# An HGRN2 trunk layer on one core: the prologue in two feature halves

## The chip, the core and the metric

The kernel runs on one core of a Trainium2 chip. The core has five engines with a queue of instructions each, worked off in order: TensorE (PE, matrix products and transposes into PSUM), VectorE (DVE, element-wise work and scans), ScalarE (ACT, activations and copies; it also issues some transfers), GpSimd (POOL, small element-wise work, memsets) and SyncE (SP, which issues transfers). The metric is the device time of one execution in microseconds, lower is better.

## The reference, cut to what matters

One layer: an HGRN2 mixer over 256 context tokens and 2048 latent tokens, then a gated ConvFFN, with adaLN modulation. The part that this case touches is the start:

```python
m_l = (silu(c) @ w_ada + b_ada)            # latent: shift, scale, gate, ... (6 x 1024)
m_c =  silu(c_ctx) @ w_ada + b_ada         # context
hl = rmsnorm(lat, norm_g0) * (1 + sc1) + sh1
hc = rmsnorm(cx,  norm_g0) * (1 + csc1) + csh1
q, f_fwd, f_bwd, v, g = split(h @ w_in)    # per head of 128 features, 8 heads
# f = lb + (1 - lb) * sigmoid(f): chunkwise linear recurrence, forward and backward;
# the latent scans start from the final state of the context scan
```

All is float32. A product is made of three fast ones: each operand is split into a rounded high part and the rest, and the kernel adds high x high, high x low and low x high.

## The kernel before, in words

The 2048 latent tokens lie in two halves of 1024 and each half in two units of 512 tokens (four tiles of 128). For each half the kernel goes over the eight heads. For a head it projects the context (in the first half only) and both units with five weight types: 2 and 1 are the gates of the two directions, 3 the values, 0 the queries, 4 the output gate. One `project` is eight feature blocks k of 128 with three products each (`step`, L442 to L448; high and low parts of the weight and of the tokens). Then come the mixer's end and the FFN, which the change leaves alone.

Before any projection the **prologue** (L200 to L309, in its own PSUM pool) makes what the projections read:

- 16 transfers of 512 KB bring the first 2048 columns of `w_ada` (shift and scale; tile `wada`), each 128 rows by 1024 columns; ACT's queue issues ten and SP's six (`ada_load`, L211). SP also brings two context tiles, the raw weights of the types (`raw`) and eight latent tiles (`x`; `stage` puts tile t into a buffer that is free by then).
- PE multiplies them with SiLU of both conditions (`silp`), 32 products in four column groups (L250, tile `mps`). ACT copies the sum (L256), PE turns it (L258, `mt`), and six small DVE instructions (L267 to L269) make the factors `A1` and shifts `B1`, for the context (index 1) and the latents (index 0).
- The normalised context is turned by PE, modulated half by ACT and half by DVE (`modulated`, L197 and L198), and split into high and low parts (`split`: ACT L78 writes the high part, DVE L79 the rest) into `cxt`.
- `normalize` of a latent tile: ACT squares and sums (L104), DVE scales (L74), POOL takes the root's inverse (L75), DVE multiplies (L109).

The first head (`head` with `first`) projects the context with types 2, 1 and 3. `unit_tok(u, k)` makes feature block k of unit u: four PE transposes, one modulation, one split into `tok`. The gates' projection of the first unit follows the blocks one by one; the second unit's tiles are normalised and its blocks are made at fixed ticks of a clock that counts steps (`at`). Then queries, values, the second unit's gates, and the first score products, ahead of which PE turns the factor `kd` (L592). I call that instruction **the meeting point**: in the program before and in the changed one the PE work ahead of it is the same work, and what follows it has the same order.

What sets the order: each engine's queue is fixed when the program is built, by the order of the code; `behind_of` keeps an instruction behind a named pair.

Of the kernel before, what the change touches and what calls it, by code (L numbers as in the profile page):

```python
# [11 lines left out]
F32 = mybir.dt.float32  # L12
# [33 lines left out]
def body(ctx, tc, a, out):  # L46
# [53 lines left out]
    def normalize(xt, junk, stp, on_act=False):  # L100

        ss = stp.tile([128, 1], F32, name="ss", tag="ss", bufs=2)
        rs = stp.tile([128, 1], F32, name="rs", tag="rs", bufs=2)
        act.activation(junk, xt, AF.Square, accum_out=ss)  # L104
        rms_scale(rs, ss, 1, D)
        if on_act:
            act.activation(xt, xt, AF.Copy, scale=rs)
        else:
            dve.tensor_scalar(xt, xt, rs, None, OP.mult)  # L109
# [69 lines left out]
    HEAD0 = (2, 1, 3, 0)  # L179
# [19 lines left out]

    with ExitStack() as c0:  # L200
        p0s = pool_(c0, "p0s", space=PSUM)
        silv = sil.rearrange("p (two k) -> p k two", two=2)
        silp = gp.tile([128, KT, 32], F32, name="silp", tag="kt", bufs=2)
        tps = [p0s.tile([128, 2, 2, 128], F32, name="tp", tag=f"tp{g}", bufs=1) for g in range(2)]
        mp = p0s.tile([128, 512], F32, name="mps")
        mt = p0s.tile([128, 4, 128], F32, name="mt")
        tps += [p0s.tile([128, 2, 2, 128], F32, name="tp", tag=f"tp{g}", bufs=1) for g in (2, 3)]
        ada = [place(i, [128, 4, D], F32, "wada") for i in range(4)]
        junk = lp.tile([128, D], F32, name="junk", tag="stg", bufs=1)

        def ada_load(q, k, i):  # L211
            n = 2 * k + i
            q.dma_start(ada[n // 4][:, n % 4], a["w_ada"][k * 128:(k + 1) * 128, i * D:(i + 1) * D])

        def raw_w(ty):
            raw = rawp.tile([128, D], F32, name="raw", tag="raw")
            sp.dma_start(raw, a["w_in"][0, ty])
            return raw

        head0 = {}  # L220

        def split_head0(ty, raw):
            head0[ty] = w = wp.tile([128, 2, KT, 128], F32R, name="w", tag="w")
            return split(w[:, 0], w[:, 1], raw.rearrange("p (k n) -> p k n", k=KT))

        pool.memset(silp, 0.0)
        stage(-2)
        stage(-1)
        for k in range(2):
            ada_load(act, k, 0)  # L230
            ada_load(sp, k, 1)
        act.activation(sil, vec[:, V_C:V_C + 16], AF.Sigmoid)
        dve.tensor_tensor(sil, sil, vec[:, V_C:V_C + 16], OP.mult)
        dve.tensor_copy(silp[:, :, 0:2], silv)
        head_raw = {}
        for k in range(2, KT):
            ada_load(act, k, 0)
            ada_load(act if k >= KT - 2 else sp, k, 1)
            if k == KT - 3:
                head_raw[2] = raw_w(2)  # L240
        head_raw[1] = raw_w(1)
        for t in range(4):
            stage(t)
        for t in (-2, -1):
            normalize(staged[t], junk, gp)
        late_junk = place(2, [128, D], F32, "junk")
        for k in range(KT):
            for c in range(4):
                n = 2 * k + c // 2
                pe.matmul(mp[32 * c:32 * c + 32], silp[:, k],  # L250
                          ada[n // 4][:, n % 4, c % 2 * 512:(c % 2 + 1) * 512],
                          start=k == 0, stop=k == KT - 1, skip_group_check=True)
        made = split_head0(2, head_raw[2])
        m2 = gp.tile([128, 512], F32, name="m2", tag="q", bufs=2)
        with behind_of(made):
            act.activation(m2, mp, AF.Copy)  # L256
        for j in range(4):
            pe.transpose(mt[:, j], m2[:, j * 128:(j + 1) * 128], ident)  # L258
        for g in range(4):
            turn_tok(tps[g], (-2, -1), (2 * g, 2 * g + 1))  # L260
        mv = mt.rearrange("p j (c r) -> p c j r", c=4)

        def by_k(v):
            return v.rearrange("p (c j) -> p c j", c=2)

        for i in (1, 0):
            dve.tensor_tensor(by_k(A1[i]), mv[:, 2:4, :, i], by_k(vec[:, V_BA + 8:V_BA + 16]), OP.add)  # L267
            dve.tensor_tensor(by_k(B1[i]), mv[:, 0:2, :, i], by_k(vec[:, V_BA:V_BA + 8]), OP.add)
            dve.scalar_tensor_tensor(A1[i], A1[i], 1.0, vec[:, V_NG:V_NG + 8], OP.add, OP.mult)  # L269
        hmc = [gp.tile([128, 2, 2, 128], F32, name="hm", tag="gv"[g % 2], bufs=2) for g in range(4)]  # L270

        def evict_ctx(g):
            return [modulated(hmc[g][:, i], tps[g][:, i], 2 * g + i, 1, i == 0).ins for i in range(2)]

        def split_ctx(g):
            b = cxt[:, g // 2, :, :, 2 * (g % 2):2 * (g % 2) + 2]
            return split(b[:, :, 0], b[:, :, 1], hmc[g].rearrange("p k s n -> p s k n"))
# [9 lines left out]
        for t in range(4, 8):  # L287
            stage(t)
# [1518 lines left out]
```

## Time and profile before

| | us |
|---|---|
| median of 3 runs (2755.13 to 2757.07) | 2755.96 |
| the profiled execution's own time | 2759.34 |
| its span, first to last instruction | 2757.3 |
| first context product (PE L445) | at 34.18 |
| meeting point (PE L592) | at 94.93 |

Times in the rows are microseconds from the span's start. A row of the timeline gives start, duration, engine, line, operation, output and inputs, sizes, how often, and in brackets the idle time of the engine just before with what ended it. PE's products overlap in its pipeline, so the distance of two starts, not the duration, is what one costs. The table of windows gives for each stretch its length, the busy time and count of PE, of its weight loads, DVE, ACT and POOL, PE's granted clock, the share of the transfer engines and GB/s.

### The profile page before, as it was taken

The numbers are of one execution on the slowest core, as the hardware profiler recorded it, in microseconds if no ns is written. First come the engines' busy times: TensorE is split into PE (matmuls) and PEld (weight loads), VectorE is DVE, ScalarE is ACT, GpSimd is POOL, SyncE is SP. The second block draws the span as 40 slices with busy tenths as digits, with TensorE's granted clock in tenths as the row PEclk, the third lists the DMA queues.
The fourth block names the chain that finished last, engine by engine and source line by source line (L and its number), as shares of the span: only waits on it lengthen the run. The fifth ranks groups of instructions, "written<-read, shape, count | busy, mean of one in ns | idle before, by whom it ended". The sixth has DMA issues, their size and how long they took to land. (4 is left out here: it accounts for less than half of the span.)

```text
span 2757.3 us, 42014 instructions
## 1 busy us (share of the span) xinstructions
PE 2708.4 (98%) x16060; PEld 2254.6 (82%) x16060; DVE 1976.0 (72%) x2791; ACT 1129.5 (41%) x1885; POOL 568.2 (21%) x885
## 2 busy tenths in 40 slices
PE   6999999999999999999999999999999999999998
PEld 4888888888888888888887888888888888877887
DVE  4756655566666776668886887777877777586886
ACT  4424443333233233335665444444444444333343
POOL 2111111011111111211220533443434440000001
PEclk9999999999999999999999999999999999999999
DMA  5213323224534443228888222228322234987563
GB/s 230 92 51 100 104 85 100 85 71 168 172 123 136 149 137 112 86 84 295 298 305 323 92 92 68 86 77 305 93 72 81 77 92 151 319 294 249 186 194 122
DMA packets 229104, 410.56 MB, mean 149 GB/s; under 512 B 29604, under 2 KB 137508, under 8 KB 225064
## 3 DMA queue, kind: packets, MB, share of 16 engines
q1 hardware_dynamic: 224584, 398.13, 43.6%
q10 hardware_dynamic: 4320, 9.77, 0.9%
q8 instruction: 126, 2.06, 0.3%
q14 instruction: 74, 0.61, 0.1%
HBM read 293.23 MB, written 114.57 MB: 148 GB/s over the span
## 5 line engine op out<-in xcount | busy, mean ns | idle before, releaser
L445 PE MATMUL z<-tok,w 128*128 128x512 f32 x1280 | 515.4, 403 | 0.0
L447 PE MATMUL z<-tok,w 128*128 128x512 f32 x1280 | 501.0, 391 | 0.0
L446 PE MATMUL z<-tok,w 128*128 128x512 f32 x1280 | 500.8, 391 | 0.0
L79 DVE TENSOR_TENSOR w<-raw,w 128x512 fp32r<-128x512 f32 (+1 forms) x260 | 239.6, 925 | 138.0 <-ACT w L78 134.0
L447 PEld LDWEIGHTS z<-tok,w 128*128 128x128 f32 x1280 | 240.4, 188 | 51.8
L445 PEld LDWEIGHTS z<-tok,w 128*128 128x128 f32 x1280 | 240.7, 188 | 46.0 <-issue 1.7
L446 PEld LDWEIGHTS z<-tok,w 128*128 128x128 f32 x1280 | 241.1, 188 | 45.0 <-DVE tok L79 0.9
L78 ACT ACTIVATE w<-raw 128x512 fp32r<-128x512 f32 (+1 forms) x260 | 196.0, 759 | 138.9 <-PE zd L1061 77.4
L1639 PE MATMUL y<-wd,ml 128*128 128x512 f32 x600 | 234.4, 391 | 2.8 <-DVE ml L79 2.7
L1637 PE MATMUL y<-wd,mh 128*128 128x512 f32 x600 | 233.8, 390 | 2.6 <-ACT X L1672 1.8
L1638 PE MATMUL y<-wd,mh 128*128 128x512 f32 x600 | 233.5, 389 | 0.0
L514 DVE TENSOR_TENSOR_SCAN S<-F,d 128x528 f32<-128x528 f32 (+1 forms) x80 | 91.5, 1143 | 113.3 <-ACT F L496 113.2
L79 DVE TENSOR_TENSOR w<-s,w 128x512 fp32r<-128x512 f32 x126 | 121.3, 968 | 52.8 <-ACT w L78 52.0
L1058 PE MATMUL zc<-rT,w 128*128 128x512 f32 x352 | 137.1, 389 | 1.2 <-DVE uv L1524 1.0
L1060 PE MATMUL zc<-rT,w 128*128 128x512 f32 x352 | 136.9, 389 | 0.0
L1061 PE MATMUL zc<-rT,w 128*128 128x512 f32 x352 | 136.9, 389 | 0.0
L1639 PEld LDWEIGHTS y<-wd,ml 128*128 128x128 f32 x600 | 112.6, 188 | 29.3 <-DVE ml L79 5.9
L1637 PEld LDWEIGHTS y<-wd,mh 128*128 128x128 f32 x600 | 112.6, 188 | 27.0 <-ACT X L1672 2.2
L78 ACT ACTIVATE w<-s 128x512 fp32r<-128x512 f32 x126 | 78.2, 627 | 137.6 <-POOL s L1114 81.0
L75 POOL TENSOR_TENSOR rs<-rs,mhalf 128x1 f32<-128x1 f32 (+3 forms) x53 | 61.7, 1165 | 345.0 <-DVE rs L74 345.0
L1638 PEld LDWEIGHTS y<-wd,mh 128*128 128x128 f32 x600 | 112.6, 188 | 23.2
L1058 PE MATMUL za<-rB,w 128*128 128x512 f32 x336 | 130.7, 389 | 0.0
(353 smaller groups left out, 6246.8 us busy)
## 6 DMA issues: line engine op xcount, KB each, us to landing
raw<-in_w_up_dram SPq DMA_DIRECT2D x88, 512.0 KB, 4.1
raw<-in_w_in_dram SPq DMA_DIRECT2D x80, 512.0 KB, 4.0
lr<-m SPq DMA_DIRECT2D x49, 512.0 KB, 6.0
m<-r SPq DMA_DIRECT2D x66, 256.0 KB, 4.1
spare<-in_w_ada_dram SPq DMA_DIRECT2D x32, 512.0 KB, 4.3
kq<-stash SPq DMA_DIRECT2D x15, 1024.0 KB, 7.8
og<-stash SPq DMA_DIRECT2D x30, 512.0 KB, 5.3
u<-in_w_down_dram SPq DMA_DIRECT2D x51, 256.0 KB, 4.2
```

What stands on the lines that cost most here:

```text
L78: i = act.activation(h, src, AF.Copy)
L79: j = dve.tensor_tensor(l, src, h.bitcast(F32), OP.subtract)
L445: pe.matmul(z, w[:, 0, k], h, start=k == 0, stop=False, skip_group_check=True)
L446: pe.matmul(z, w[:, 0, k], l, start=False, stop=False, skip_group_check=True)
L447: pe.matmul(z, w[:, 1, k], h, start=False, stop=k == KT - 1, skip_group_check=True)
L514: dve.tensor_tensor_scan(flat(S[:, d]), flat(F[:, d]), flat(d1[:, 0:ns]), 0.0, OP.mult, OP.max)
L1058: pe.matmul(o, w[:, 0, k], r[:, :, 0, k], start=start and k == 0, stop=False, skip_group_check=True)
L1060: pe.matmul(o, w[:, 0, k], r[:, :, 1, k], start=False, stop=False, skip_group_check=True)
L1061: pe.matmul(o, w[:, 1, k], r[:, :, 0, k], start=False, stop=k == 3, skip_group_check=True)
L1637: pe.matmul(z, lh, rh, start=start, stop=False, skip_group_check=True)
L1638: pe.matmul(z, lh, rl, start=False, stop=False, skip_group_check=True)
L1639: pe.matmul(z, ll, rh, start=False, stop=stop, skip_group_check=True)
```

## The change

The separate prologue is gone. A new function `first_head` does the prologue and the first head together, in two halves of the feature blocks, k = 0 to 3 and k = 4 to 7:

- `w_ada` comes in 16 transfers of the same size, cut by columns: first the eight that make the first 512 columns of shift and of scale, each as two runs of 512 columns in a row, then after raw weight 2, four latent tiles and raw weight 1 the other eight. ACT's queue issues two, SP's 14.
- Modulation products have 256 columns in place of 512 and are twice as many, in two sums (`mods`, `mod_rows`). Eight products of the second half stand between the projections of the first.
- After the first half's factors, the context's first two blocks of two and the first unit's blocks 0 to 3 are made and projected with types 2 and 1 (sums stay open in PSUM); after the second half's, the rest. The context's values, its scan and the normalising of the second unit's tiles come after that.
- Gates of the context: one sigmoid for both directions, in place in PSUM. The small work on the lower bounds (L301 to L309) and POOL's memsets change places in POOL's queue, so that `silp` is cleared later. The score tiles `sc` are cleared after the modulation sums, which use their PSUM.

The diff, cut:

```diff
-        for k in range(KT):
-            for c in range(4):
-                n = 2 * k + c // 2
-                pe.matmul(mp[32 * c:32 * c + 32], silp[:, k],
-                          ada[n // 4][:, n % 4, c % 2 * 512:(c % 2 + 1) * 512],
-                          start=k == 0, stop=k == KT - 1, skip_group_check=True)
...
-        made = evict_ctx(0)
-        order = [(evict_ctx, 1), (split_ctx, 0), (evict_ctx, 2), (split_ctx, 1), (split_head0, 1),
-                 (evict_ctx, 3), (split_ctx, 2), (split_ctx, 3)]
...
-        places = ("kv", "o", "tr")
+        places = (("tr", "kv", "o", "tr") * 2, ("kv", "o", "tr") * 3)
...
-                for i in range(UT):
-                    at(clock[0] + 1 + 2 * i, lambda i=i: more(UT + i))
-                for k in range(KT):
-                    at(clock[0] + 10 + 2 * k, lambda k=k: unit_tok(1, k))
...
+            def ada_load(q, k, hf):
+                q.dma_start(ada[2 * hf + k // 4][:, k % 4],
+                            a["w_ada"][k * 128:(k + 1) * 128, 0:2 * D].rearrange(
+                                "p (i c) -> p i c", i=2)[:, :, hf * 512:(hf + 1) * 512])
...
+            for k in range(KT):
+                ada_load(act if k in (0, 2) else sp, k, 0)
+            raw_w(2)
+            for t in range(4):
+                stage(t)
+            raw_w(1)
+            for k in range(KT):
+                ada_load(sp, k, 1)
...
+            def mods(hf, k):
+                for c in range(4):
+                    pe.matmul(mps[hf][32 * c:32 * c + 32], silp[:, k],
+                              ada[2 * hf + k // 4][:, k % 4, c // 2,
+                                                   c % 2 * 256:(c % 2 + 1) * 256],
+                              start=k == 0, stop=k == KT - 1, skip_group_check=True)
...
+            def ctx_steps(d, hf):
+                for k in range(4 * hf, 4 * hf + 4):
+                    step(zc[:, d], w[2 - d], cxt[:, hf], k, hf == 1, d == 0)
+
+            def unit_steps_(k):
+                for d, z in enumerate(zs):
+                    step(z, w[2 - d], block(0, k // 4), k, k >= 4)
+
+            mod_rows(0)
+            then(evict_ctx, 0)
+            then(evict_ctx, 1)
+            then(split_ctx, 0)
+            then(split_head0, 2)
+            then(split_ctx, 1)
+            ctx_steps(0, 0)
+            mods(1, 0)
+            for t in range(4):
+                then(normalize, staged[t], junk, gp)
+            then(split_head0, 1)
+            ctx_steps(1, 0)
+            mods(1, 1)
+            then(unit_tok, 0, 0)
+            for k in range(4):
+                if k < 3:
+                    then(unit_tok, 0, k + 1)
+                mods(1, 2 + k)
+                unit_steps_(k)
+            raw_w(3)
+            raw_w(0)
+            for t in range(4, 8):
+                stage(t)
...
+            mods(1, 6)
+            mods(1, 7)
+            turn_ctx(2)
+            turn_ctx(3)
+            mod_rows(1)
+            for f, n in ((evict_ctx, 2), (evict_ctx, 3), (split_ctx, 2), (split_ctx, 3)):
+                then(f, n)
+            then(unit_tok, 0, 4)
...
+            for i in range(UT):
+                at(clock[0] + 15 + 2 * i, lambda i=i: more(UT + i))
+            for k in range(KT):
+                at(clock[0] + 23 + 2 * k, lambda k=k: unit_tok(1, k))
+            for d in range(2):
+                ctx_steps(d, 1)
+            for k in range(4, KT):
+                if k + 1 < KT:
+                    then(unit_tok, 0, k + 1)
+                if k == 6:
+                    then(split_head0, 3)
+                unit_steps_(k)
...
+            then(split_head0, 0)
+            ckd, csd = factors(h, None, None, None)
+            cv, turn = values(project(w[3], None), 2)
```

What this does to the queues, at the three places that matter below. `mps` is a modulation sum, `mt` the turned sum, `tp` a turned tile, `z` a projection's sum; the number behind `x_` tells the token tiles apart.

PE, the modulation products, before:

```order
L250 MATMUL mps<-wada,silp 32x512 x32
L193 MATMUL tp<-ident,x_166 128x128 x4
L258 MATMUL mt<-ident,m_249 128x128 x4
L193 MATMUL tp<-ident,x_168 128x128
L193 MATMUL tp<-ident,x_166 128x128
```

and PE in the change, around the end of the second half's products:

```order
L881 MATMUL mps<-wada,silp 32x256 x4
L330 MATMUL z<-tok,w 128x512
L331 MATMUL z<-tok,w 128x512
L332 MATMUL z<-tok,w 128x512
L330 MATMUL z<-tok,w 128x512
L331 MATMUL z<-tok,w 128x512
L332 MATMUL z<-tok,w 128x512
L881 MATMUL mps<-wada,silp 32x256 x8
L192 MATMUL tp<-ident,x_195 128x128
```

The last two modulation products of the second half stand behind the projection of block 3, so the second half's factors wait for that projection, and not only for `w_ada`.

DVE after the last split of the first unit's blocks, in the change (L400 is the scan of `factors`, L407, L408 and L426 what it makes, L109 a tile of the second unit being normalised, L79 on `w` a weight being split):

```order
L79 TENSOR_TENSOR w<-raw,w 128x1024
L74 TENSOR_SCALAR rs<-ss 128x1
L109 TENSOR_SCALAR x_461<-x_461,rs 128x1024
L400 SCALAR_TENSOR_TENSOR S<-F_169,d_165 128x264
L407 TENSOR_TENSOR ke<-S 128x256
L400 SCALAR_TENSOR_TENSOR S<-F_169,d_165 128x264
L408 TENSOR_TENSOR ke<-S 128x8x32
L426 TENSOR_TENSOR kd<-ke,TB_173 128x2x256
L400 SCALAR_TENSOR_TENSOR S<-F_168,d_165 128x528
L79 TENSOR_TENSOR w<-raw,w 128x1024
L400 SCALAR_TENSOR_TENSOR S<-F_168,d_165 128x528
L74 TENSOR_SCALAR rs<-ss 128x1
```

and the same place before, where the first unit's scan (L514) comes when the context's scan, both weights and all the second unit's tiles are done:

```order
L74 TENSOR_SCALAR rs<-ss 128x1
L109 TENSOR_SCALAR x_310<-x_310,rs 128x1024
L79 TENSOR_TENSOR tok<-hm,tok 128x4x128
L79 TENSOR_TENSOR w<-raw,w 128x1024
L198 TENSOR_SCALAR hm<-tp,A_0_113,B_0_115 128x512
L79 TENSOR_TENSOR tok<-hm,tok 128x4x128
L198 TENSOR_SCALAR hm<-tp,A_0_113,B_0_115 128x512
L79 TENSOR_TENSOR tok<-hm,tok 128x4x128 x2
L198 TENSOR_SCALAR hm<-tp,A_0_113,B_0_115 128x512
L79 TENSOR_TENSOR tok<-hm,tok 128x4x128 x2
L514 SCALAR_TENSOR_TENSOR S<-F_372,d_369 128x528
```

Work that stood ahead of the first unit's gates on DVE stands behind them now. On POOL the inverse roots (L75) of the second unit's tiles stood in one piece ahead of the first unit's small factors, and stand now between and behind them:

```order
L414 COPY TB_172<-S 128x2x4
L418 COPY TB_172<-S 128x2x4
L434 COPY TX_174<-S 128x4
L435 COPY TX_174<-S 128x4
L75 TENSOR_TENSOR rs<-rs,mhalf 128x1
L415 TENSOR_TENSOR TB_172<-TB_172,S 128x2x4
L419 TENSOR_TENSOR TB_172<-TB_172,S 128x2x4
L416 TENSOR_TENSOR TB_172<-TB_172,S 128x2x4
L420 TENSOR_TENSOR TB_172<-TB_172,S 128x2x4
L417 TENSOR_TENSOR sd<-TB_172,S 128x8
L432 COPY decb<-sd 128x4
L75 TENSOR_TENSOR rs<-rs,mhalf 128x1 x3
```

The roots of three tiles (two of the second unit, the last a later one) stand behind the copy into `decb`.

259 lines of the change are left out of this document (128 added, 131 removed).

## The prediction

> **What bounds the kernel now.** I read the page's busy times first, then the windows of the first 100 us, then the timelines of PE and DVE there.
>
> ```profile
> PE 2708.4 (98%) x16060; PEld 2254.6 (82%) x16060; DVE 1976.0 (72%) x2791; ACT 1129.5 (41%) x1885; POOL 568.2 (21%) x885
> 20.00:30.00 10.00, 6.55 (x36) 1.05 (x28) 2.20 (x4) 2.77 (x5) 0.91 (x2) 0.83 1.02 408
> 30.00:40.00 10.00, 7.00 (x46) 5.13 (x43) 7.86 (x19) 7.35 (x13) 0.39 (x2) 1.00 0.92 349
> 40.00:50.00 10.00, 7.53 (x54) 6.92 (x54) 7.51 (x15) 6.90 (x14) 3.33 (x11) 0.91 0.33 108
> 72.37:94.93 22.56, 22.56 (x108) 18.60 (x107) 19.17 (x29) 13.31 (x22) 6.63 (x13) 1.00 0.17 59
> 31.85:91.42 59.57, 53.67 (x295) 43.89 (x294) 48.59 (x86) 39.39 (x68) 11.94 (x28) 0.97 0.27 96
> ```
>
> PE is busy 98% of the span, so a prologue can give back only what PE idles early. Until 30 us the transfers run at full share and DVE and ACT have little to do; from 72.37 to the meeting point at 94.93 PE has no pause. In between, DVE is busy 48.59 of 59.57 us and waits the other 11.0.
>
> ```profile
> 16.97 1.93 PE L250 MATMUL mps<-wada,silp 128*32 128x512 f32 x8 [0.61 <-DMA wada<-in_w_ada_dram]
> 29.41 1.05 PE L250 MATMUL mps<-wada,silp 128*32 128x512 f32 x4 [1.10 <-DMA wada<-in_w_ada_dram]
> 34.18 0.38 PE L445 MATMUL z<-cxt,w 128*128 128x256 f32 x1 [1.06 <-ACT cxt L78]
> 94.93 0.60 PE L592 MATMUL tr<-ident,kd 128*128 128x128 f32 x4
> 31.85 0.17 DVE L267 TENSOR_TENSOR A<-mt,vec 128x8 f32<-128x8 f32 x1 [0.88 <-PE mt L258]
> 90.73 0.69 DVE L583 TENSOR_TENSOR ke<-ke,rt 128x512 f32<-128x512 f32 x1
> ```
>
> The last modulation product waits for the last piece of w_ada at 29.41 and ends at 30.46; DVE's factors follow at 31.85, the first context product at 34.18. At the other end DVE is done at 91.42, 3.5 us ahead of the meeting point: there PE is the bound, not DVE. All work ahead of the meeting point is kept, so the change is worth what it shifts that point.
>
> **The first half's load.** Behind the constants and the context (1.11 MB) come 4.19 MB in rows of 2 KB in place of 4 KB.
>
> ```profile
> GB/s 0 126 366 410 421 423 415 421 399 410 412 404 418 404 407 423 401 410 415 404 412 407 410 421 347 85 292 265 107 292 11 0 0 5 0 0 0 5 0 0
> DMA packets 1133, 4.12 MB, mean 412 GB/s; under 512 B 128, under 2 KB 128, under 8 KB 1133
> q1 hardware_dynamic: 4320, 7.87, 36.3%
> q1 hardware_dynamic: 2533, 5.38, 81.2%
> ```
>
> The first row (0 to 60 us, 1.5 us a number) moves 1.35 MB by 6.0, so context and constants are in at 5.4. The second is the w_ada stream from 10 to 20 us: 412 GB/s. The third and fourth are stretches of mostly 2 KB packets: 7.87 MB in 36.3% of 57 us from 2700, 380 GB/s while busy; and 5.38 MB in 81.2% of 20 us from 2480, 331. I take 380, whose packets are 2 KB almost alone: 11.0 us, landed at 16.4 (bounds 15.6 and 18.1). [...]
>
> A modulation block of 512 columns took 1.93 (16.97 row), half as many columns take 1.0: 17.4. From there to DVE's first factor it was 1.4; a copy of half the width and two turnings in place of four save 0.3: **18.5 in place of 31.85**.
>
> Moved past these loads on SP: raw weight 2 lands at 17.7, the four tiles to 22.8, weight 1 at 24.0, the second half of w_ada from 25.4 to 35.1, then weights 3 and 0 and four tiles to 42.7 (1.27 each at 412, 1.38 in 2 KB rows). PE comes to the last piece of the second half behind block 3, at 39.8 below: 4.7 spare, so this load is hidden. POOL's later clearing of silp, about 8 us, is hidden by the stream too: two pieces have landed then, and PE takes 1.0 a piece where one comes every 1.38; uncovered it would cost 3. ACT is freed from issuing.
>
> **DVE's way to the meeting point.** From 18.5 its work is the same 48.6 us (six small additions more, tenths). I laid the measured durations end to end in the changed queues, each instruction when its engine is free and its inputs are made. The waits on DVE come from these rows:
>
> ```profile
> 43.71 0.15 DVE L74 TENSOR_SCALAR rs<-ss 128x1 f32<-128x1 f32 x1
> 44.58 0.75 DVE L109 TENSOR_SCALAR x<-x,rs 128x1024 f32<-128x1024 f32 x1 [0.72 <-POOL rs L75]
> 45.25 0.15 DVE L74 TENSOR_SCALAR rs<-ss 128x1 f32<-128x1 f32 x1
> 47.29 0.78 ACT L197 ACTIVATE hm<-tp,B,A 128x512 f32<-128x512 f32 x1 [1.96 <-PE tp L193]
> 49.78 0.63 ACT L78 ACTIVATE tok<-hm 128x512 fp32r<-128x512 f32 x1 [1.05 <-DVE hm L198]
> 51.26 0.78 ACT L197 ACTIVATE hm<-tp,B,A 128x512 f32<-128x512 f32 x1 [0.85 <-DVE tok L79]
> 48.63 0.45 POOL L528 COPY TB<-S 128x4 f32<-128x4 f32 x1 [2.55 <-DVE S L514]
> 49.79 0.21 POOL L531 TENSOR_TENSOR sd<-TB,S 128x4 f32<-128x4 f32 x1
> 92.66 0.39 PE L447 MATMUL z<-tok,w 128*128 128x512 f32 x1
> 92.89 0.39 PE L445 MATMUL z<-tok,w 128*128 128x512 f32 x1
> ```
>
> - Two context halves: three waits of a third of a us, 1.0.
> - Roots of the first unit's four tiles on POOL, 0.7 each: 2.8.
> - Blocks 0 to 3: DVE waits for ACT's split, ACT for DVE's modulation, in turn (47.29 to 51.26 is one round), five waits of 0.4 to 0.8: 3.5. In the prologue before, other DVE work filled some of these. Blocks 4 to 7 again: 3.9.
> - Between the halves: with block 3 split at 37.7, PE does its projection (0.23 a product, 92.66 to 92.89), the last two modulation blocks (about 0.55 each at full clock), copy and turning; DVE's second factors come at 41.5. A new wait of 3.7, and behind it queue the second context half and blocks 4 to 7.
> - After block 7 (52.8): weight 3 0.3, four tiles' roots 1.9, kd behind POOL's small factors (48.63 to 50.00, 1.4 long) 1.2, the rest 1.2: 4.6.
>
> Sum 19.5 where before it was 11.0. So DVE ends the second unit's last split at 18.5 + 48.6 + 19.5 = 86.6, and since that split is now last, 16 gate products of 0.23 stand behind it: meeting point at **90.4**, 4.5 early on paper. The early start (13.4) goes into 8.5 of waits, and the bound passes from PE to DVE.
>
> Three things take the rest back. First, such a laying is short: done for the kernel before from 30.46 it reaches the meeting point at 92.6, not 94.93, 2.3 in 62 us; over 73 us that is 2.7. Second, POOL:
>
> ```profile
> 81.01 2.91 POOL L546 COPY decb<-sd 128x4 f32<-128x4 f32 x1
> 104.39 0.49 PE L693 MATMUL o<-states,qi 128*128 128x128 f32 x2 [0.77 <-DVE states L674]
> ```
>
> The copy into decb took 2.91 beside DVE's scans. It delayed nobody; now two roots of the second unit stand behind it, DVE waits for them with the scans behind, and PE for the turned tiles. I laid 0.5; the bounds are 0 and 2.4 more, and I take 0.8, since the scans that stretched it now come after. Third, PE's clock:
>
> ```profile
> 41.01 0.28 PE L445 MATMUL z<-cxt,w 128*128 128x256 f32 x1
> 41.13 0.28 PE L446 MATMUL z<-cxt,w 128*128 128x256 f32 x1
> 50.42 0.41 PE L445 MATMUL z<-cxt,w 128*128 128x256 f32 x1
> 50.63 0.41 PE L446 MATMUL z<-cxt,w 128*128 128x256 f32 x1
> L250 PE MATMUL mps<-wada,silp x64: 592/1058/1063, 5.2 to 29.9; 128*32 128x512 f32 x64
> ```
>
> The same product costs 0.12 at 41 us and 0.21 at 50, after three thin microseconds; modulation products take 592 ns or 1058. In the change PE is thinly used from 17.4 to 28.6 and then full to 39.8 with 0.6 spare, so slow products there delay the second half. Bounds 0 and 9 (below); I take 1.2. [...]
>
> Sum: -4.5 + 2.7 + 0.8 + 1.2 = +0.2. Behind the meeting point the program is the same; PE's wait at 104.39 could shrink, which I count as 0 to -1.1 and take as 0, since DVE is no further ahead. Against the profiled span that is 2757.5 after 2757.3; the shown runs' median, 2755.96, gives **2756.2**. About 0.2%, 5.5 us, is what a measurement of this kernel tells from no change, so the forecast is: no change.
>
> **Rivals.** *PE stays the bound (faster, 0.24).* If DVE's waits stay near 11, PE sets the end: the first unit's gates done at 53.3 on paper, then 96 products of 0.23, 24 of 0.12, some 42 turnings and the context's state (4.7 together), 29.7: 83.0, with 2.4 for the laying and 1.2 for the clock 86.6. That is 8.3 early, 2747.6. For it: PE has no wait after 72.37, and DVE was 3.5 ahead. Against it: DVE has 29 us of work left behind block 7, where the blocks' end before left it 19. The two ends on paper, 90.4 for DVE and 83.0 for PE, are 7 us apart, and most of DVE's 19.5 us of waits is read from rows of another order; so this is a quarter.
>
> *PE stays slow between the halves (slower, 0.26).* In 28.6 to 39.8 PE does 24 unit products (5.5), six modulation blocks (2.7) and ten context products (1.2). All at half rate costs 9.4 less 0.6 spare: 8.8 for the second half and all behind it. Then the sum is +7.8, 2763.8. It decides, past 5.5, when more than about 7.1 us of this work is slow. For it: the modulation products of before, with PE busy three quarters of the time, stayed at 1058 ns for most of 25 us. Against it: this stretch has nearly no idle time, where before every modulation block waited for its piece of w_ada.
>
> *The halving brings nothing because the load is late (inside the forecast).* At 331 GB/s the first half lands 1.7 later and the sum is 1.9, 2757.9; the second half is still covered.
>
> **Chances.** Forecast 0.50, of which 0.03 falls past the bound on the fast side and 0.05 on the slow. With the rivals: faster 0.27, same 0.42, slower 0.31. The forecast's own range: low with the fast load, no POOL or clock loss, a laying short by 2.0 and the wait at 104.39 gone, -4.5 - 0.8 + 2.0 - 1.1 = -4.4, 2751.6; high with 2.4 of POOL, 3.4 of clock and the slow load, -4.5 + 2.7 + 2.4 + 3.4 + 1.7 = +5.7, 2761.7. The rivals on both sides hold half the chance, so the range reaches a little past the time of each, which I take to hold six tenths of it: 2746.5 to 2764.5, with 0.2 left out.
>
> **What will show it.** The last piece of the first half should land near 16.4; DVE's first factors near 18.5, second near 42 to 44; block 7 split near 54 to 56; PE with waits between 53 and 85 for DVE (second unit's tiles and splits) where it had none; the meeting point near 95. DVE's waits up to it should be near 20. I am wrong on DVE if PE runs unbroken after the first unit's gates; wrong on the clock if products at 30 to 40 us stand 0.43 apart throughout; wrong on the load if modulation blocks of the second half wait for w_ada behind block 3.

## The result, and the profile after

| | before | changed |
|---|---|---|
| median of 22 runs each, us | 2756.49 | 2759.68 |
| lowest to highest | 2754.09 to 2759.22 | 2756.61 to 2763.78 |
| span of the profiled execution | 2757.3 | 2757.8 |
| first factors (DVE) | 31.85 | 22.78 |
| meeting point | 94.93 | 98.19 |

The ratio is 1.0014, with an interval of 1.0008 to 1.0020: 0.14% slower, inside what was forecast as no change. The early start came (9.1 us of it, not 13.4), and by the meeting point all of it was gone and 3.3 us more. The first line has the busy times of the changed kernel's page, the rest is PE's timeline.

```profile
PE 2705.9 (98%) x16124; PEld 2255.1 (82%) x16124; DVE 1982.4 (72%) x2797; ACT 1129.4 (41%) x1885; POOL 574.4 (21%) x885
...
15.60 0.39 PE L192 MATMUL tp<-ident,x 128*128 128x128 f32 x1
18.04 0.99 PE L192 MATMUL tp<-ident,x 128*128 128x128 f32 x7 [2.05 <-DVE x L109]
18.96 2.62 PE L881 MATMUL mps<-wada,silp 128*32 128x256 f32 x24
...
44.89 1.07 PE L881 MATMUL mps<-wada,silp 128*32 128x256 f32 x16
...
67.81 0.50 PE L332 MATMUL z<-tok,w 128*128 128x512 f32 x1 [1.77 <-DVE w L79]
...
71.35 0.66 PE L192 MATMUL tp<-ident,x 128*128 128x128 f32 x4 [1.42 <-DVE rs L74]
...
98.19 0.60 PE L478 MATMUL tr<-ident,kd 128*128 128x128 f32 x4
...
106.72 0.48 PE L579 MATMUL o<-states,qi 128*128 128x128 f32 x2
```

Two things are seen. Ahead of the first factors PE stops between the first and the second of the context's turnings (`tp`), and the last 24 modulation products of the first half stand behind that and start at 18.96. Behind block 7 PE waits for DVE (1.77, 1.42 and others), where before it ran without a pause from 72.37. DVE's and POOL's rows say why PE stopped at 16 us:

```profile
11.05 0.77 DVE L109 TENSOR_SCALAR x<-x,rs 128x1024 f32<-128x1024 f32 x1
17.14 0.17 DVE L872 TENSOR_TENSOR lbw<-lbw 128x16 f32<-128x16 f32 x1 [5.33 <-POOL lbw L871]
17.24 0.74 DVE L109 TENSOR_SCALAR x<-x,rs 128x1024 f32<-128x1024 f32 x1
...
22.78 0.16 DVE L899 TENSOR_TENSOR A<-mt,vec 128x4 f32<-128x4 f32 x1 [4.34 <-PE mt L891]
...
47.24 0.16 DVE L899 TENSOR_TENSOR A<-mt,vec 128x4 f32<-128x4 f32 x1 [4.37 <-PE mt L891]
...
58.05 0.69 DVE L79 TENSOR_TENSOR tok<-hm,tok 128x512 fp32r<-128x512 f32 x1 [0.70 <-ACT tok L78]
...
93.38 0.69 DVE L79 TENSOR_TENSOR tok<-hm,tok 128x512 fp32r<-128x512 f32 x1 [0.70 <-ACT tok L78]
```

```profile
11.61 5.50 POOL L871 TENSOR_TENSOR lbw<-lbw 128x32 f32<-128x32 f32 x1
```

POOL's power for the lower bounds (L871) takes 5.50 us. On DVE its consumer L872 stands ahead of the scaling of the second context tile (L109 at 17.24), and that tile's turning stands ahead of modulation products 5 to 7 on PE. Of this chain only L872 and the three small instructions behind it need the power. In the kernel before the same power ran in the open:

```profile
4.87 5.46 POOL L305 TENSOR_TENSOR lbw<-lbw 128x32 f32<-128x32 f32 x1 [3.03 <-DVE sil L233]
```

```profile
10.37 0.17 DVE L306 TENSOR_TENSOR lbw<-lbw 128x16 f32<-128x16 f32 x1 [5.21 <-POOL lbw L305]
...
20.70 0.15 DVE L74 TENSOR_SCALAR rs<-ss 128x1 f32<-128x1 f32 x1 [9.45 <-ACT junk L104]
```

DVE stood still for it there too, 5.21 us, but its next work came at 20.70.

The window of the changed kernel from the first factors to the second unit's last split, then DVE's waits by what ended them (us in total, times, longest), first after and then before, and last DVE's splits of weights in the two windows, first before and then after:

```profile
22.78:94.07 71.29, 59.64 (x354) 44.15 (x355) 50.39 (x93) 41.70 (x70) 12.37 (x28) 0.95 0.38 138
```

```profile
DVE A L899 <- PE mt L891: 8.7, 2, 4.4
DVE tok L79 <- ACT tok L78: 6.4, 10, 0.8
DVE x L109 <- POOL rs L75: 6.2, 8, 1.2
```

```profile
DVE x L109 <- POOL rs L75: 4.9, 7, 0.7
...
DVE tok L79 <- ACT tok L78: 3.1, 3, 1.4
```

```profile
L79 DVE TENSOR_TENSOR w<-raw,w 128x1024 fp32r<-128x1024 f32 x3 | 3.7, 1220 | 0.2 <-ACT w L78 0.2
```

```profile
L79 DVE TENSOR_TENSOR w<-raw,w 128x1024 fp32r<-128x1024 f32 x4 | 4.9, 1217 | 0.5 <-ACT w L78 0.5
```

DVE needs 71.29 us from its first factors to the last split where it needed 59.57: it is busy 50.39 in place of 48.59, and waits 20.9 in place of 11.0. Of the waits, 4.4 are the second factors' (half of the 8.7; the other half is the first factors', at the edge of the stretch), 3.3 more are splits waiting for ACT, 1.3 more POOL's roots. Of the 1.8 us more work, 1.2 is a weight's split: before, type 2 was split at 28.27, ahead of the first factors, and now it is split behind them. Most of the rest is the six small additions.

### The profile page after: what moved, and what is told of

Same layout as the page of the kernel before. It is cut to its first block, busy times and chain, and to the rows that moved or that the text cites. A ratio compares the mean times of both kernels' runs of the same rounds, so it can differ in the third digit from the quotient of the medians.

```text
span 2757.8 us, 42145 instructions
## 1 busy us (share of the span) xinstructions
PE 2705.9 (98%) x16124; PEld 2255.1 (82%) x16124; DVE 1982.4 (72%) x2797; ACT 1129.4 (41%) x1885; POOL 574.4 (21%) x885
## 4 chain that ended last, share of the span: by engine, by line
PE 70%; DMA 6%; DVE 4%; issue 2%; ACT 1%; SPq 0%; POOL 0%; ACTq 0%; DVEq 0%; POOLq 0%
PE z L330 7%; PE z L332 7%; PE z L331 7%; PE za L1126 3%; PE za L1123 3%; PE za L1125 3%; PE zd L1123 3%; PE zc L1123 3%; PE zd L1126 3%; PE zc L1126 3%; PE zd L1125 3%; PE zc L1125 3%; PE y L1704 2%; PE y L1702 2%; PE y L1703 2%
## 5 line engine op out<-in xcount | busy, mean ns | idle before, releaser
L79 DVE TENSOR_TENSOR w<-raw,w 128x512 fp32r<-128x512 f32 (+1 forms) x260 | 239.2, 923 | 132.5 <-ACT w L78 128.6
L400 DVE TENSOR_TENSOR_SCAN S<-F,d 128x528 f32<-128x528 f32 (+1 forms) x80 | 91.4, 1143 | 113.4 <-ACT F L382 113.4
L79 DVE TENSOR_TENSOR w<-s,w 128x512 fp32r<-128x512 f32 x126 | 125.0, 997 | 48.1 <-ACT w L78 47.5
L75 POOL TENSOR_TENSOR rs<-rs,mhalf 128x1 f32<-128x1 f32 (+3 forms) x53 | 62.8, 1186 | 357.1 <-DVE rs L74 357.1
```

The costliest lines, as they stand in the source:

```text
L79: j = dve.tensor_tensor(l, src, h.bitcast(F32), OP.subtract)
L400: dve.tensor_tensor_scan(flat(S[:, d]), flat(F[:, d]), flat(d1[:, 0:ns]), 0.0, OP.mult, OP.max)
```

## The experiments

Each kernel's trace gives three marks that are sharper than its time: the first factors, the second factors and the meeting point. Up to the meeting point PE does the same work in all of them (one adds dummy products), so a shift there, counted from the first factors, is what an edit brought behind them. The first factors themselves are less sharp: the changed kernel, e2 and e3 are the same program up to there, and have them at 21.02 to 22.78. The times spread by up to 7 us within one kernel; in e9, the one kernel with two profiles, the way from the first factors to the meeting point repeats to 0.2. The ratios are to the kernel before on the same chip; the chips differ from one group of experiments to the next.

| kernel | first factors | second factors | meeting point | first factors to meeting point | median, us | ratio to before (interval) |
|---|---|---|---|---|---|---|
| before | 31.85 | | 94.93 | 63.08 | | |
| changed | 22.78 | 47.24 | 98.19 | 75.41 | 2759.68 | 1.0014 (1.0008 to 1.0020) |
| e1 power late | 19.49 | 44.03 | 95.02 | 75.53 | 2754.04 | 0.9999 (0.9990 to 1.0009) |
| e2 modulation early | 22.34 | 47.11 | 98.11 | 75.77 | 2757.94 | 1.0013 (1.0003 to 1.0022) |
| e3 tiles in the gap | 21.02 | 45.92 | 95.34 | 74.32 | 2756.37 | 1.0004 (0.9994 to 1.0013) |
| e4 warm | 24.57 | 49.04 | 99.96 | 75.39 | 2757.54 | 1.0006 (0.9996 to 1.0015) |
| e5 = e1 + products late | 19.28 | 41.78 | 93.46 | 74.18 | 2754.07 | 1.0001 (0.9992 to 1.0011) |
| e6 = e1 + two blocks | 19.21 | 43.63 | 94.57 | 75.36 | 2754.37 | 1.0001 (0.9991 to 1.0011) |
| e7 = e1 + sums ahead | 18.86 | 43.33 | 95.25 | 76.39 | 2756.05 | 1.0008 (0.9999 to 1.0018) |
| e8 = e1 + e3 | 19.34 | 45.24 | 95.78 | 76.44 | 2754.92 | 1.0002 (0.9992 to 1.0012) |
| e9 = e5 + tiles spread | 18.90 | 41.34 | 91.56 | 72.66 | 2752.03 | 0.9993 (0.9985 to 1.0002) |
| e10 = e9 + e6 | 19.60 | 42.04 | 92.03 | 72.43 | 2754.69 | 0.9996 (0.9987 to 1.0005) |
| e11 = e9 + unit early | 19.61 | 42.07 | 91.58 | 71.97 | 2753.52 | 0.9997 (0.9988 to 1.0006) |
| e9 again | 19.18 | 41.62 | 92.04 | 72.86 | 2752.42 | 0.9991 (0.9982 to 1.0001) |

### e1: the power's consumers later

```diff
-            dve.tensor_tensor(mx, e2[:, 0], e2[:, 1], OP.add)
-            dve.reciprocal(mx, mx)
-            dve.tensor_tensor(lb, e2[:, 0], mx, OP.mult)
-            dve.tensor_tensor(oml, e2[:, 1], mx, OP.mult)
             for t in (-2, -1):
                 normalize(staged[t], junk, gp)
...
             mod_rows(0)
+            dve.tensor_tensor(mx, e2[:, 0], e2[:, 1], OP.add)
+            dve.reciprocal(mx, mx)
+            dve.tensor_tensor(lb, e2[:, 0], mx, OP.mult)
+            dve.tensor_tensor(oml, e2[:, 1], mx, OP.mult)
```

> In the changed kernel DVE waits from 11.8 to 17.1 us for POOL's 5.50 us power of the lower bounds (L871) ahead of scaling the second context tile; PE's turning of that tile stands ahead of modulation products 5 to 7 of the first half. Here DVE's use of the power (L872 to L875) stands behind that scaling. Theory: the first factors come at 19 to 20 instead of 22.78 and the meeting point at 95 to 95.5 instead of 98.19, the time 2.5 to 3.2 us below the changed kernel's. Rival (the first half's load or PE's low clock sets the first factors): they stay above 21.5 and the meeting point above 97.5.

DVE's rows, then PE's:

```profile
10.74 1.60 DVE L109 TENSOR_SCALAR x<-x,rs 128x1024 f32<-128x1024 f32 x2
16.84 0.17 DVE L941 TENSOR_TENSOR lbw<-lbw 128x16 f32<-128x16 f32 x1 [4.50 <-POOL lbw L871]
```

```profile
15.29 1.62 PE L192 MATMUL tp<-ident,x 128*128 128x128 f32 x8
16.83 1.68 PE L877 MATMUL mps<-wada,silp 128*32 128x256 f32 x24
```

Both context tiles are scaled in one go, DVE's wait for the power has nothing behind it, and PE's turnings and products follow without a pause. First factors 3.3 earlier, meeting point 3.2 earlier, as the theory has it; the ratio to the kernel before goes from 1.0014 to 0.9999, with intervals that just touch. The meeting point is back where it was before the change (95.02 and 94.93), so in this profile the one place in two queues accounts for what the changed kernel loses there.

The 3.3 has two parts. The last 24 products start 2.1 earlier (16.83 against 18.96), and they take 1.68 in place of 2.62: in the changed kernel the granted clock was 0.50 from 19.2 on, in e1 it was 1.00. The second part is not always there. In the nine profiles with this edit (e1, e5 to e11, e9 again) the first factors stand at 18.86 to 19.61, in the three without it at 21.02 to 22.78, so the place costs 1.4 to 3.9, by the profile.

### e2: the second half's modulation products earlier

```diff
-                mods(1, 2 + k)
+                if k < 2:
+                    for j in range(3):
+                        mods(1, 2 + 3 * k + j)
                 unit_steps_(k)
...
-            mods(1, 6)
-            mods(1, 7)
```

> The eight modulation blocks of the second half all stand ahead of the last two projections of the first unit's blocks 0 to 3. Theory (DVE waits 4.4 us at the second factors because of PE's queue, and DVE bounds what follows): the second factors at 42.9 to 44 instead of 47.24, the meeting point 3 to 4 earlier, at 94 to 95. Rival (PE is the bound behind the second factors, so products put off are paid there): second factors earlier, meeting point at 97 to 98.2.

```profile
43.05 0.64 PE L881 MATMUL mps<-wada,silp 128*32 128x256 f32 x8
...
45.82 1.03 PE L192 MATMUL tp<-ident,x 128*128 128x128 f32 x8
46.69 0.38 PE L891 MATMUL mt<-ident,m 128*128 128x128 f32 x2
```

The theory did not come, and of the rival only the late meeting point (98.11), without earlier second factors. The last modulation products end at 43.7 in place of 46.0, but the sum is turned (L891) at 46.69, behind nine products of the projections and eight turnings that PE had put off. PE ran without a pause from 34 to 47 us, so moving work about inside this stretch changes nothing. What stands ahead of the turning has to become less: e5.

### e3: two tiles of the second unit in the gap

```diff
+            for i in range(2):
+                order[0] = more(UT + i)
             mods(1, 6)
             mods(1, 7)
             turn_ctx(2)
             turn_ctx(3)
-            mod_rows(1)
+            with behind_of(order[0]):
+                mod_rows(1)
...
-            for i in range(UT):
+            for i in range(2, UT):
                 at(clock[0] + 15 + 2 * i, lambda i=i: more(UT + i))
```

> Two of the second unit's tiles are normalised between block 3 and the second factors, in DVE's wait of 4.4 us, in place of later. Theory (DVE bounds the stretch to the meeting point): the second factors at most 0.5 later than 47.24, the two normalisings (0.15 + 0.75 + about 0.8 of waiting for POOL each, 3.4 together) are gone from the later stretch, meeting point at 95 to 96. Rival (PE is the bound there): meeting point unchanged, 97.7 to 98.7.

```profile
44.13 0.75 DVE L109 TENSOR_SCALAR x<-x,rs 128x1024 f32<-128x1024 f32 x1 [0.73 <-POOL rs L75]
45.92 0.16 DVE L899 TENSOR_TENSOR A<-mt,vec 128x4 f32<-128x4 f32 x1 [1.04 <-PE mt L891]
```

The two tiles fit, with 1.04 of the wait left, but only 1.1 of the 3.4 us came back on the way from the first factors. The rest of the 2.85 at the meeting point is an earlier first factor, 21.02 against 22.78, in a kernel that is the same up to there; more on that in the last section.

### e4: PE kept warm

28 dummy modulation products, no part of the computation, into a spare PSUM tile.

```diff
                 if k == 4:
                     turn_ctx(0)
+                    dummy(2)
                     turn_ctx(1)
...
             mod_rows(0)
+            dummy(5)
```

> 28 more modulation products into a spare PSUM tile in PE's two early waits (8 ahead of the turning of the second context tile, 20 behind the first factors' turning), so that PE has less idle time before the first context products. They are no part of the computation. Theory (DVE paces this stretch, so the clock costs nothing): the first context products stand nearer 0.12 than 0.21 apart, the meeting point stays within 0.5 of 98.19. Rival (the low clock delays the second half, my term of 1.2 to 3.4): meeting point 1.2 to 3.4 earlier.

```profile
24.57:30.11 5.54, 3.81 (x44) 2.42 (x44) 4.46 (x13) 4.95 (x8) 0.31 (x1) 1.00 1.04 385
30.20:33.50 3.30, 3.30 (x23) 1.12 (x21) 1.66 (x5) 3.24 (x7) 1.25 (x3) 0.50 1.05 387
```

```profile
26.00:33.00 7.00, 6.54 (x34) 4.21 (x34) 4.30 (x9) 5.89 (x10) 2.01 (x4) 0.51 1.05 387
```

The first fence is e4: clock 1.00 from its first factors through its first context products, which stand 0.12 apart as the theory has it, and 0.50 only behind them. The second is the changed kernel at that place: 0.51 throughout. So in e4's profile 3.3 us stand at half clock there, and 6.8 (26.0 to 32.8) in the changed kernel's. The dummies delay the first factors by 1.8, and with them the meeting point, which the forecast of 98.19 left out. From the first factors on it takes 24.47 to the second factors against 24.46, and 75.39 to the meeting point against 75.41: these 3.5 us at half clock cost nothing. In both kernels PE waits at the end of the slow stretch for a tile that DVE scales (0.23 in e4, 0.19 in the changed kernel), so DVE sets the pace there.

### e5: less PE work ahead of the second factors

```diff
-                mods(1, 2 + k)
-                unit_steps_(k)
+                for j in ((2, 3, 4), (5,), (6, 7), ())[k]:
+                    mods(1, j)
+                if k == 0:
+                    unit_steps_(k)
...
+            mod_rows(1)
             turn_ctx(2)
             turn_ctx(3)
-            mod_rows(1)
+            for k in range(1, 4):
+                unit_steps_(k)
```

> On top of the late power (first factors 19.49, second 44.03, meeting point 95.02 in that kernel): modulation products of the second half earlier, and the first unit's products of blocks 1 to 3 behind the second sum in the program, so that PE turns that sum with 14 products ahead of it in place of 24. Theory (with modulation products earlier alone PE was unbroken up to the second factors, so the amount of PE work ahead of them sets them, and DVE bounds what follows): second factors 2.3 earlier, 41.3 to 42.2, meeting point 92.5 to 93.5. Rival (the products put off are paid for behind, where PE is the bound): second factors earlier, meeting point at 94.5 to 95.3.

```profile
51.19 0.69 DVE L79 TENSOR_TENSOR tok<-hm,tok 128x512 fp32r<-128x512 f32 x1 [2.39 <-ACT tok L78]
```

Second factors 2.25 earlier than in e1, as the theory has it; meeting point 1.6 earlier, at 93.46, inside its range. The 0.7 between them is paid in blocks 4 to 7, where DVE waits 2.39 once for a block whose turning stands behind the products put off.

### e6 and e10: two blocks in flight

```diff
             def then(f, *args):
+                after = ahead[0] if f is unit_tok and args[1] not in (0, 4) else order[0]
+                ahead[0] = order[0]
```

> On top of the late power: a block of the first unit is kept behind the block before the last instead of behind the last, so that DVE modulates block 1 (and 5) ahead of the split of block 0 (and 4) and ACT need not wait for it. Theory (the turn-taking of ACT and DVE in the two groups of four blocks is on the way to the meeting point): blocks 0 to 3 end about 0.7 earlier, which the second factors' wait takes up, blocks 4 to 7 about 0.7 to 1.5 earlier, meeting point 93.5 to 94.4. Rival (PE's turning and the projections behind the second factors pace the blocks): meeting point 94.6 to 95.4.

> e9 with the block order of e6, which alone took 0.2 off the way to the meeting point. Theory of e6 (turn-taking is on the way): 0.7 to 1 earlier than e9. Rival (blocks are paced by PE's turnings and the tiles behind them): within 0.3 of e9.

From the first factors to the meeting point it brings 0.2 in both (75.53 to 75.36, 72.66 to 72.43): what the rival says, though e6's 94.57 itself falls between the two ranges. Counted from the first factors, block 1 ends 1.5 earlier in e6, but the last of each four only 0.1. In e6 PE's clock was down for a while:

```profile
65.30:72.20 6.90, 6.21 (x20) 4.49 (x19) 4.35 (x10) 1.42 (x3) 5.51 (x14) 0.51 0.19 71
```

That is 6.9 us at half clock in the stretch behind block 7. e10 had no such stretch there and gained as little, so the low clock cost next to nothing.

### e7: sums and roots one tile ahead

```diff
-            for t in range(4):
-                then(normalize, staged[t], junk, gp)
+            then(stat, 0)
+            for t in range(4):
+                if t < 3:
+                    then(stat, t + 1)
+                then(scale, t)
```

> On top of the late power: a tile's sum and inverse root are made ahead of the scaling of the tile before it, so that DVE does not stand still for POOL's root four times (0.73 each). Theory (DVE's waits for roots delay the tiles' turning, and PE is unbroken from there to the second factors): the first unit's scalings end 1.4 earlier, the second factors 1 to 1.4 earlier (42.6 to 43.0), meeting point 93.6 to 94.1. Rival (the second factors hang on the load or on PE alone): second factors at 43.7 to 44.1, meeting point at 94.7 to 95.3.

```profile
24.80 0.15 DVE L958 TENSOR_SCALAR rs<-ss 128x1 f32<-128x1 f32 x1 [0.85 <-ACT junk L957]
```

```profile
26.29 1.08 PE L877 MATMUL mps<-wada,silp 128*32 128x256 f32 x8 [0.45 <-DMA wada<-in_w_ada_dram]
```

The theory fails in this profile. The last scaling starts 0.85 earlier after the first factors (9.6 against 10.45) and not 1.4, since DVE now waits for ACT's sums in place of most of POOL's roots, and none of it arrives: second factors 24.5 after the first, as in e1. PE's row says why. In e7 and in e1 PE waits for `w_ada` 7.4 after the first factors (0.45 and 0.44) and then runs without a pause to the second factors, so a tile that is ready earlier finds PE busy. PE was at half clock there, up to 28 us: the eight products of the row took 1.08, where eight at clock 1.00 took 0.64 (at 34.39 in the changed kernel). In four profiles in which the half clock ended sooner (e6, e9, e10, e9 again) PE does wait for such a tile, 0.60 to 0.76, so what the earlier scalings bring at full clock stays open. The part behind the second factors took 0.9 longer, with PE's clock down in it:

```profile
73.00:80.00 7.00, 7.00 (x38) 5.93 (x37) 6.05 (x12) 5.40 (x9) 0.00 (x0) 0.80 0.01 2
```

PE has no pause in these 7 us. That the clock is the reason for the 0.9 is likely here, and was not tried. In e4 the clock was 0.50 from 71.5 to 77.5, with pauses of PE, and its way to the meeting point was no longer.

### e8: the gap with e1

The edits of e1 and e3 together.

> On top of the late power: two tiles of the second unit normalised ahead of the second factors. Alone it took 1.1 off the way from the first factors to the meeting point. Theory (the two changes add up, since they take waits from different places): first factors 19.5, second 43.9 to 44.5, meeting point 93.7 to 94.2. Rival (the tiles now land too late for the earlier gap: in the changed kernel the last of the four landed at 43.2): second factors at 45 or later, meeting point at 94.8 or later.

```profile
40.96 1.06 ACT L104 ACTIVATE junk<-x 128x1024 f32<-128x1024 f32 x1 [2.06 <-DMA x<-in_x_dram]
```

```profile
42.15 0.15 DVE L74 TENSOR_SCALAR rs<-ss 128x1 f32<-128x1 f32 x1 [2.51 <-ACT junk L104]
```

The rival: with everything 3 us earlier the tiles have not landed. ACT waits 2.06 for the first of them, DVE 2.51 for ACT's sum, and the second factors behind it come at 45.24.

### e9: the tiles spread among blocks 4 to 7

```diff
-                at(clock[0] + 15 + 2 * i, lambda i=i: more(UT + i))
+                at(clock[0] + (8, 12, 15, 17)[i], lambda i=i: more(UT + i))
```

> On top of e5 (second factors 41.78, meeting point 93.46): two of the second unit's four tiles are normalised among blocks 4 to 7, where DVE waits for ACT's splits, instead of behind block 7, where they stand behind POOL's small factors. Theory (DVE's waits behind block 7, four roots of POOL, are the part of its waits that other work can take up): block 7 at most 1 later, meeting point 1.5 to 2.5 earlier, 91 to 92, and the time about 2 below e5's. Rival (ACT, busy 9 of 14 us among blocks 4 to 7, takes 2.5 more there and delays the blocks by as much): meeting point at 93 to 94.

> The kernel of e9 a second time, for its time and for what is the same in a second profile. Theory: second factors to meeting point 50.2 again within 0.3, meeting point 91 to 92.5, median 2751 to 2753, 2 to 4 below the kernel before. Rival (the gain in the time was chance, and the profile's start does not carry to the end): median within 1 of the kernel before, meeting point off by more than 1 from 91.56.

The windows from the end of block 7's split to the meeting point, e9 and then e5:

```profile
54.31:91.56 37.25, 32.55 (x170) 25.93 (x171) 30.49 (x48) 21.45 (x37) 8.19 (x22) 1.00 0.19 64
```

```profile
53.99:93.46 39.47, 33.12 (x175) 26.16 (x175) 31.17 (x52) 24.26 (x42) 10.16 (x24) 1.00 0.18 61
```

Block 7 ends 0.8 later after the second factors than in e5, and the rest takes 2.2 less, so the way from the first factors is 1.5 shorter, and 1.3 in the second profile: the theory, both times. Two sets of runs give 2752.03 and 2752.42, 3.4 and 3.0 below the kernel before on the same chip. Each interval still just takes in 1, so about 0.1% faster than the kernel before is likely and not proved; both intervals stand clear of that of the changed kernel.

### e11: the second unit's blocks three steps earlier

```diff
-                at(clock[0] + 23 + 2 * k, lambda k=k: unit_tok(1, k))
+                at(clock[0] + 20 + 2 * k, lambda k=k: unit_tok(1, k))
```

> e9 with the second unit's blocks made three steps earlier (20 instead of 23). Theory (DVE ends with the second unit's last split, and 16 gate products stand behind it; an earlier split lets PE run through): last split 1 to 2 earlier than in e9, meeting point 1 to 2 earlier. Rival (DVE's amount of work sets both, and what is put off, the score factors, is then late for the meeting point): meeting point within 0.5 of e9 or later, PE waiting for kd or the score operands.

```profile
95.12 0.66 PE L478 MATMUL tr<-ident,kd 128*128 128x128 f32 x4 [1.66 <-ACT kt L480]
```

The last split comes 2.1 earlier counted from the first factors (85.41 less 19.61 against 86.77 less 18.90), as the theory has it. The meeting point comes only 0.7 earlier, between the two forecasts, and then PE waits 1.66 for the next turning's operand: work that was put off is late. What is gained ahead of the meeting point is lost right behind it: the first product of L579 stands 82.2 after the first factors, in e9 81.2.

## Why the prediction was right, step by step

The outcome, no change within 0.2%, was right, and so was the main reason: DVE takes over as the bound behind block 7, and its waits eat the early start. The sum was less good than the outcome. Its +0.2 was 3.1 short at the meeting point, its terms partly cancel, and the forecast's room of 5.5 us on either side took in the rest: that much is luck. Of the signs that it named, the second factors (42 to 44), block 7 (54 to 56) and the meeting point (95) all came about 3 late, at 47.24, 58.74 and 98.19. Counted from the first factors the first two were forecast 23.0 and 34.3 later and came 24.5 and 36.0 later, so most of the error is in the first factors.

- **The first factors, 18.5: wrong, they came at 22.78.** This is the step that failed: "From there to DVE's first factor it was 1.4; a copy of half the width and two turnings in place of four save 0.3". The way from load to factors was priced by its four steps alone, as if nothing else stood in the queues there. The section on the change names the lower bounds' work as moved in POOL's queue, and the prediction gave it no price. In e1 it was worth 3.3 at the first factors and 3.2 at the meeting point, of which 0.9 is slower products. Without it the nine profiles are 0.4 to 1.1 over 18.5, no more than the load is late.
- **The load: 0.9 to 1.6 too early.** In the five profiles in which PE was ahead of it (e6, e7, e9, e10, e11), the wait ends at 17.25 to 18.00 in place of 16.4, between the bounds of 15.6 and 18.1. The row is e9's; in the changed kernel itself PE came too late to wait for it.

```profile
17.28 0.64 PE L877 MATMUL mps<-wada,silp 128*32 128x256 f32 x8 [0.71 <-DMA wada<-in_w_ada_dram]
```

- **The clearing of `silp`, about 8, hidden: overlooked in part.** POOL cleared it by 7.5, but on DVE the copy into it stands behind an instruction of the second context tile (L74), which waited for ACT, so PE began at 11.17 (DVE's rows, then PE's). It can have cost little: in those five profiles PE began about as late, at 10.55 to 11.02, and still had to wait for the load. No run moved it.

```profile
10.86 0.15 DVE L74 TENSOR_SCALAR rs<-ss 128x1 f32<-128x1 f32 x1 [2.25 <-ACT junk L104]
10.94 0.17 DVE L861 COPY silp<-sil 128x16 f32<-128x16 f32 x1
```

```profile
11.17 4.50 PE L881 MATMUL mps<-wada,silp 128*32 128x256 f32 x40 [11.17 <-DVE silp L861]
```

- **The second half's load hidden: right in the changed kernel.** No modulation product of it waits for `w_ada`; PE comes to the last at 44.89. In e1 and e6 to e11, with the first factors some 3 us earlier, the first of them waits 0.44 to 0.47.
- **The new wait at the second factors: right in kind.** 3.7 forecast, 4.37 measured. That PE's amount of work ahead of them causes it, e2 and e5 show together.
- **DVE's work, "the same 48.6 us": 1.8 too little.** The 48.6 is a window with three weight splits, and from its first factors on the changed kernel has four; that is 1.2, and the six small additions are most of the rest.
- **DVE's waits, 19.5 and 2.7 for the laying: right in sum.** 20.9 of waits were measured. The last split came 71.29 after the first factors; 68.1 on paper, 71.6 with the 2.7 and POOL's 0.8. The 2.7 also had to cover the 1.8 of work that the sum had missed, which is luck. Splits wait twice as long for ACT as before (6.4 against 3.1), where other work had filled some of these waits.
- **POOL's 0.8: about right in size, for another reason.** The copy into `decb` took 0.19, not 2.91. Before, it started at 81.01, 1.7 ahead of the scans (82.69), so it is not shown that they stretched it. Behind block 7 DVE waits 3.3 for four roots (0.73, 0.97, 1.20 and 0.38), where 1.9 and the 0.8 were forecast. The roots stand behind and between the other small work that POOL does for the factors:

```profile
70.47 0.22 POOL L415 TENSOR_TENSOR TB<-TB,S 128x8 f32<-128x8 f32 x1
...
72.43 0.19 POOL L432 COPY decb<-sd 128x4 f32<-128x4 f32 x1
72.57 0.55 POOL L75 TENSOR_TENSOR rs<-rs,mhalf 128x1 f32<-128x1 f32 x1
```

- **The clock, 1.2: wrong in place.** In the changed kernel the clock was 0.50 from 26.0 to 32.8 and 1.00 from there to the second factors, and e4, with 3.5 us less of it, was no faster behind the first factors (75.39 to the meeting point, 75.41 in the changed kernel). The half clock that was paid for was ahead of the first factors: 24 products took 2.62 there and 1.68 in e1. The 3.4 of clock in the range's high end, which is also the upper figure of e4's rival, was the author's assumption, and no run shows it: the losses measured are this 0.9, and none for the 3.5 us that e4 has less.
- **16 gate products behind the last split: right.** 94.07 to 98.19 is 4.1, forecast 3.8.
- **The wait at 104.39: taken as 0, it was worth 0.9.** Before it stood at 104.39 for 0.77; the same product (L579) has none at 106.72, so that 3.26 at the meeting point is 2.33 behind it.

Add the 4.3 that the first factors were late, take off the clock's 1.2 and this 0.9, and +0.2 becomes +2.4; the traces stand 2.3 apart at 107 us. That it fits so closely rests on the smaller errors above, which cancel. The medians are 3.2 apart, and their interval (2.2 to 5.5) takes in 2.3.

Of the rivals, PE as the bound is out (PE waits for DVE behind block 7). Slow products are out by the changed kernel's own trace: from 36.59 on the products of block 0 stand 0.23 apart. That the load is late is true, but in the changed kernel no product waited for it.

## What to carry to other kernels

When a small instruction moves in one in-order queue, find its consumer in the other queue and what stands behind that consumer: here 128x16 numbers that nobody needed for 40 us held up 128x1024 that all else waited for (DVE stood still 5.33 us), and the cure was to write four lines further down. An early start is worth only what the engine that bounds the stretch behind it can use, so its waits have to be shortened (e5) or filled with other work (e9), after seeing that the work's inputs have landed (e8) and that the engine ahead has room (e2, e7). Shifts between two traces at an instruction with the same work ahead of it tell tenths of a us where medians tell whole ones, if they are counted from a mark behind the part that differs by chance.

## What the runs showed of the hardware that was not expected

POOL's power took 5.50 us for 128x32 and, in most rows, 0.55 for 128x1 (28.01 to 32.63 in the changed kernel; up to 1.43 at 74.05). As an estimate from these two sizes, each further column costs some 0.16 ((5.50 - 0.55) / 31). POOL's product of 128x8 at 70.47 took 0.22 in all.

PE's clock falls at different places in two profiles of the same instructions. e2 and e3 are the same program up to the first factors, and ran the same 24 products from 18.5 us, the first at half clock and the second at full:

```profile
18.53:21.32 2.79, 2.79 (x25) 0.99 (x24) 0.00 (x0) 0.00 (x0) 0.00 (x0) 0.50 1.04 416
```

```profile
18.54:20.04 1.50, 1.50 (x25) 0.68 (x24) 0.00 (x0) 0.00 (x0) 0.00 (x0) 1.00 1.06 421
```

That is 1.3 us in the first factors by chance (22.34 and 21.02). In both PE had waited 2 us shortly ahead of them (2.11 and 1.97); in the nine profiles without that wait (e1, e5 to e11, e9 again) the clock was 1.00 there each time. What sets the place is not shown. In the changed kernel, behind a wait of 2.05, the same 24 products took 2.62, where e2 took 2.79 and e3 1.50: there, one profile has 1.3 us that another has not.
